# First norm of a hybrid layer: four selecting matmuls in a row, later strips recorded between the first products, twelve idle matmuls

## The chip, the cores and the metric

The kernel runs on one core of one Trainium2 chip. The metric is the device time of one execution in microseconds, the median of the runs shown. A profile of one further execution gives the rows used here.

## The reference

One layer of a bidirectional hybrid model works on 640 tokens of width 1024: 128 of a prompt and 512 of a sample. All matrices are float32. What matters for this change is the beginning:

```python
def layer(x, mod, p, lru_h0, gla_s0, rows):
    sh1, sc1, g1, sh2, sc2, g2 = jnp.split(mod, N_MOD, axis=-1)
    ng = p['norm_g']
    h = rmsnorm(x, ng[0]) * (1.0 + sc1) + sh1
    m, s_lru, s_gla = token_mix(h, p, lru_h0, gla_s0, rows)
    x = x + g1 * rmsnorm(m, ng[1])
    h = rmsnorm(x, ng[2]) * (1.0 + sc2) + sh2
    f = jnp.square(jax.nn.relu(h @ p['mlp_w1'])) @ p['mlp_w2']
    x = x + g2 * rmsnorm(f, ng[3])
```

Here `mod` is `silu(c) @ w_mod + b_mod`, once with the prompt's conditioning vector and once with the sample's; `w_mod` is 1024 by 6144. `token_mix` begins with `z = h @ p['w_in']` (1024 by 7200); its first 1024 columns feed a convolution and a recurrence.

## The kernel before, in words

**Layout.** The normed input h lies transposed, features on partitions, in eight column blocks k of 128 features by 640 tokens. Every product is made of three float32r matmuls, so h is kept as a high part (tile HH) and a remainder (tile HL), and every weight block as `whi` (a cast on ScalarE) and `wlo` (a subtraction on VectorE).

**The first norm.** Each of the five token tiles is loaded, squared and summed on ScalarE, scaled on VectorE, and transposed on TensorE into the tiles `xnT`. Then each column block k needs a scale column `a1` and a shift column `sh1` for both conditioning vectors. They come from two strips of 256 columns of `w_mod` for every two blocks, a "pair" n: `mod_load` loads a strip as four tiles `modw` of 256 KB, `mod_pair(n)` multiplies them with the conditioning vectors in sixteen matmuls (two rows of the profile each, as every float32 matmul), copies the sums to the tile `rw`, and gathers the columns with four selecting matmuls against `sel`, each followed by an add on VectorE into `a1` or `sh1`. `make_h(k)` scales block k (128 tokens on VectorE, 512 on ScalarE) and splits it into HH and HL.

**The first unit.** The input projection starts with three column blocks of `w_in` together (`N_FIRST`), with k as the outer loop: `first_part(k)` issues the products of block k for all three, 6 matmuls of 320 columns each. The three accumulate in two `dense` tiles and one `aux` tile of PSUM; there are two of each kind. `prep` loads weights (1 MB for two blocks, at most two such loads open) and splits them.

**The order.** Nothing is issued as it is written. A recorder keeps all operations with their dependencies; `order` is a list scheduler over all engines and the DMA queue, with a cost for each operation. An engine that comes free takes, among the instructions that are ready by the plan, the one of the lowest rank, which is the number of its recording less `rec.ahead`; it does not wait for one that will be ready soon. Weight splits are recorded with `rec.ahead = SPLIT_AHEAD` (50). A PSUM tile counts as one region, so that an engine's access waits for another engine's earlier accesses anywhere in the tile. The plan fixes the order on each engine; on the chip, each engine works through it and waits on semaphores. `startup` records the first norm after the letters of `MIX`: x a token tile's transposes, l the load of a strip, d and D weight loads, m a pair, p the first weight splits, h two blocks of h.

Of the kernel before, what the change touches and what calls it, by code (L numbers as in the profile page):

```python
# [39 lines left out]
POOL_OUT = (5,)  # L40
G2_FROM = 6
N_WARM = 24

EARLY = "xxxrxxmm"
MIX = "XdllxxxxxDllmphllmhmhmh"
N_FIRST = 3


# [6 lines left out]
def _dims(ap):  # L57
    n = 1
    for _, k in ap.ap[1:]:
        n *= k  # L60
    return n
# [48 lines left out]
class Recorder:  # L110
# [114 lines left out]
    def order(self):  # L225
# [20 lines left out]
        table, dma_free, seq, out, busy = None, 0.0, 0, [], {}  # L246
# [3 lines left out]
        while len(out) < len(ops):  # L250
            best = None
            for e in engs:
                if avail[e]:
                    t = free[e]
                elif future[e]:
                    t = max(free[e], future[e][0][0])
                else:
                    continue
                if best is None or t < best[0]:
                    best = (t, e)  # L260
            assert best, "no instruction can go on"
            t, e = best
            while future[e] and future[e][0][0] <= t:
                i = heapq.heappop(future[e])[1]
                heapq.heappush(avail[e], ops[i].rank)
            if e == "ACT" and table is not None:
                r = min(avail[e], key=lambda r: r[0] + (self.SWITCH_AGE if ops[r[1]].table not in (None, table) else 0))
                avail[e].remove(r)
                heapq.heapify(avail[e])
            else:  # L270
                r = heapq.heappop(avail[e])
            i = r[1]
            o = ops[i]
            wait, block = t, None
            fresh = [nm for nm in o.tiles if nm not in got]
            for tag in {self.tile_of[nm] for nm in fresh}:
                mine = [nm for nm in fresh if self.tile_of[nm] == tag]
                before = due[tag].index(max(mine, key=rank.get)) + 1
                if len(slots[tag]) < before:
                    block = tag  # L280
                else:
                    wait = max(wait, heapq.nsmallest(len(mine), slots[tag])[-1])
            if block:
                held[block].append(i)
                continue
            if wait > t:
                heapq.heappush(future[e], (wait, i))
                continue
            for nm in fresh:
                tag = self.tile_of[nm]  # L290
                got.add(nm)
                due[tag].remove(nm)
                heapq.heappop(slots[tag])
                for j in held[tag]:
                    heapq.heappush(future[ops[j].eng], (t, j))
                held[tag] = []
            us = o.us
            if o.table and o.table != table:
                us += self.SWITCH_US
                table = o.table  # L300
            if e == "PE":

                w = int(t / self.WINDOW_US)
                if busy.get(w - 1, 0.0) < 0.375 * self.WINDOW_US:
                    us *= 2
                if _dims(o.kw["out"] if "out" in o.kw else o.args[0]) >= 64:
                    busy[w] = busy.get(w, 0.0) + o.us
            o.at, o.seq = t, seq
            seq += 1
            free[e] = t + us  # L310
            o.done = t + us
            if o.name == "dma_start":
                dst = o.kw["out"]
                size = dst.ap[0][1] * _dims(dst) * 4
                onchip = o.kw["in_"].space == bass.MemoryType.SB
                dma_free = max(dma_free, t + us + 0.6) + size / 360e3
                o.done = dma_free + (1.25 if onchip else 0.9)
            out.append(o)
            for u in o.users:
                u.ready = max(u.ready, o.done + self.lag(e, u.eng))  # L320
                u.waits -= 1
                if not u.waits:
                    heapq.heappush(future[u.eng], (u.ready, u.idx))
            for nm in o.tiles:
                left[nm] -= 1
                if not left[nm]:
                    tag = self.tile_of[nm]
                    heapq.heappush(slots[tag], o.done + 0.1)
                    for j in held[tag]:
                        heapq.heappush(future[ops[j].eng], (t, j))  # L330
                    held[tag] = []
# [60 lines left out]
def tile_hybrid_layer(  # L392
# [7 lines left out]
    rec = Recorder(nc)  # L400
    V, A, PE, G, SP = (Port(rec, e) for e in ("DVE", "ACT", "PE", "POOL", "SP"))
# [13 lines left out]
    def t_(name, dt=F32):  # L415
        return rec.tile(tp, N_T, [128, TW], dt, name, "t")
# [4 lines left out]
    def dense():  # L421
        return rec.tile(psd, 2, [128, 2, 512], F32, "dense", "d")

    def aux():
        return rec.tile(psa, 2, [128, 2, 512], F32, "aux", "a")
# [14 lines left out]
    def copy(e, dst, src):  # L440
        A.copy(dst, src) if e == "A" else by[e].tensor_copy(dst, src)
# [15 lines left out]
    ident = consts.tile([128, 128], F32, name="ident")  # L457
# [19 lines left out]
    def load_rows(rows, q):  # L477
        for dst, r0, n, src in rows:
            q.dma_start(out=dst[r0:r0 + n, :], in_=src)
# [40 lines left out]
    ps = aux()  # L520
    for _ in range(N_WARM):
        PE.matmul(ps[:, 0, 0:128], ident, ident, start=True, stop=True)
# [19 lines left out]
    ps = aux()  # L542
# [6 lines left out]
    sel = consts.tile([128, 2], F32, name="sel")  # L549
# [82 lines left out]
    def mod_pair(n):  # L632


        ps = aux()

        for m in (1, 0):
            for r in (1, 0):
                for j in (3, 2, 1, 0):
                    k = 4 * r + j  # L640
                    PE.matmul(ps[32 * j:32 * (j + 1), m, 0:256], cst32[:, k, :], modw[2 * n + m][k // 2][:, k % 2, :],
                              start=r == 1, stop=r == 0)
        rw = t_("rw")
        A.copy(rw[:, 0:512].rearrange("p (m c) -> p m c", m=2), ps[:, :, 0:256])
        for m in range(2):
            for i in range(2):
                k = 2 * n + i
                pc = ps[:, m, 256 + 2 * i:258 + 2 * i]
                PE.matmul(pc, rw[:, 256 * m + 128 * i:256 * m + 128 * (i + 1)], sel, start=True, stop=True)
                if m:  # L650
                    V.tensor_scalar(cols["sh1"][:, :, k], pc, bm(0, k), None, op0=OP.add)
                else:
                    V.tensor_scalar(cols["a1"][:, :, k], pc, bm1[:, k:k + 1], ng(0, k), op0=OP.add, op1=OP.mult)

    xnT = []
    HH = rec.tile(big, 1, [128, 8, T], F32R, "HH", "hh")
# [8 lines left out]
    def make_h(k):  # L665
        x = xnT[k]
        for e, i, sl in zip(MH_ENG, range(2), (slice(0, 128), slice(128, T))):
            scaled(e, x[:, sl], x[:, sl], cols["a1"][:, i, k:k + 1], cols["sh1"][:, i, k:k + 1])
        copy(MH_ENG[2], HH[:, k, :], x[:, 0:T])
        by[MH_ENG[3]].tensor_tensor(HL[:, k, :], x[:, 0:T], f32(HH[:, k, :]), op=OP.subtract)  # L670
# [37 lines left out]
    def startup():  # L708
        ps = aux()
        PE.transpose(ps[:, 0, 0:80], v2[0:80, :], ident[0:80, 0:80])  # L710
        V.tensor_copy(C2, ps[:, 0, 0:80])
        V.tensor_scalar(bm1, bmv(1), 1.0, None, op0=OP.add)
        for t in range(NT):
            x_norm(t)
        load_rows(rows_etc, G)
        ps = aux()
        PE.transpose(ps[:, 0, 0:114], v1[0:114, :], ident[0:114, 0:114])
        V.tensor_copy(C1, ps[:, 0, 0:114])
        nm = nx = nh = 0
        for s_ in MIX:  # L720
            if s_ == "l":
                modw.append(mod_load(len(modw)))
            elif s_ == "m":
                mod_pair(nm)
                nm += 1
            elif s_ == "X":
                xnT.extend(t_(f"xnT{k}") for k in range(KT))
            elif s_ == "p":
                prep(0, 0, 0)
            elif s_ == "h":  # L730
                for k in (2 * nh, 2 * nh + 1):
                    make_h(k)
                nh += 1
            elif s_ in "dD":
                do_loads(1 if s_ == "d" else 2)
            else:
                x_T(nx, dense())
                nx += 1


    def fm_mm(ps, piece, xh, xl, c0, c1, ks, k_all=KT):
# [69 lines left out]
    def first_part(k):  # L811
        if k == 0:
            first_ps.extend([dense(), dense(), aux()])
        for u, p in enumerate(pzx[0:N_FIRST]):
            fm_mm(first_ps[u], p, hh, hl, 0, T, (k,))

# [1029 lines left out]
```

## Time and profile before

| | us |
|---|---|
| median of three runs | 1134.96 |
| lowest, highest run | 1134.83, 1137.45 |
| the profiled execution | 1134.4 |
| its span, first to last instruction | 1132.6 |

The profile is of one execution. Busy times count the instructions that the profiler saw on an engine; the end of a matmul is modelled, and matmuls overlap in the pipeline. All operations are issued by one helper line, L343, so that rows are told apart by their tiles.

### The profile page before, as it was taken

How to read it: one execution, taken by the hardware profiler on the slowest of the kernel's cores; microseconds unless marked ns; L12 is line 12 of the kernel's file. 1: busy time of each engine (PE TensorE's matmuls, PEld its weight loads, DVE VectorE, ACT ScalarE, POOL GpSimd, SP SyncE). 2: the span in 40 equal slices, each digit the busy share in tenths (PEclk: the TensorE clock that was granted, in tenths of full speed). 3: DMA queues.
4: the chain of work that ended last, by engine and by line, in shares of the span. 5: the costliest groups of instructions: out<-in, count | busy, mean ns of one | idle time of the engine just before them, and what ended most of it. 6: DMA issues, size and time to landing. Idle time of an engine off the chain costs nothing.

```text
span 1132.6 us, 17807 instructions
## 1 busy us (share of the span) xinstructions
PE 1106.1 (98%) x7020; PEld 1039.9 (92%) x7020; DVE 847.7 (75%) x1359; ACT 615.7 (54%) x998; POOL 78.7 (7%) x151
## 2 busy tenths in 40 slices
PE   6999999999999999999999999999999999999997
PEld 5799899999999999999999888888998988889896
DVE  4686885968474738628997569997779989987767
ACT  5377989895575758512443258754434433333452
POOL 3136103000000000000000021000000000000001
PEclk8999999999999999999999999999999999999999
DMA  9835436241321212226544456322233333222522
GB/s 293 269 73 152 123 83 176 69 132 38 95 75 57 75 57 75 90 76 235 176 158 168 143 196 207 124 76 75 75 129 128 101 124 134 94 75 75 154 88 93
DMA packets 104475, 136.94 MB, mean 121 GB/s; under 512 B 8178, under 2 KB 78020, under 8 KB 104392
## 3 DMA queue, kind: packets, MB, share of 16 engines
q1 hardware_dynamic: 102200, 133.65, 38.0%
q0 software_dynamic: 2048, 1.90, 0.7%
q8 instruction: 55, 0.90, 0.3%
q10 hardware_dynamic: 144, 0.26, 0.1%
q14 instruction: 28, 0.23, 0.1%
HBM read 121.61 MB, written 6.31 MB: 113 GB/s over the span
## 4 chain that ended last, share of the span: by engine, by line
PE 81%; DVE 6%; ACT 6%; DMA 4%; issue 2%; SPq 0%; POOL 0%; DVEq 0%; POOLq 0%; ACTq 0%
PE dense L343 55%; PE aux L343 26%; DVE i L343 2%; DMA modw<-in_w_mod_dram 1%; DVE th L343 1%; ACT L343 1%; DMA i<-r 1%; DVE wlo L343 1%; DMA raw<-in_w_in_dram 1%; ACT r L343 1%; ACT whi L343 1%; ACT th L343 1%; DMA xb<-in_x_sample_dram 0%; ACT L342 0%; DVE ab L343 0%
## 5 line engine op out<-in xcount | busy, mean ns | idle before, releaser
L343 ACT CAST whi<-raw 128x1024 fp32r<-128x1024 f32 (+2 forms) x173 | 167.0, 969 | 290.3 <-PE aux L343 140.3
L343 DVE TENSOR_TENSOR wlo<-raw,whi 128x1024 fp32r<-128x1024 f32 (+1 forms) x168 | 190.2, 1133 | 75.9 <-ACT whi L343 74.9
L343 PE MATMUL dense<-HH,whi 128*128 128x320 f32 x768 | 177.7, 311 | 0.2 <-ACT vc L343 0.2
L343 PE MATMUL dense<-HL,whi 128*128 128x320 f32 x768 | 175.9, 309 | 0.0
L343 PE MATMUL dense<-HH,wlo 128*128 128x320 f32 x752 | 172.4, 309 | 0.0
L343 PEld LDWEIGHTS dense<-HH,whi 128*128 128x128 f32 x768 | 128.2, 188 | 1.9 <-issue 0.6
L343 PEld LDWEIGHTS dense<-HL,whi 128*128 128x128 f32 x768 | 128.6, 188 | 0.0
L343 PEld LDWEIGHTS dense<-HH,wlo 128*128 128x128 f32 x752 | 125.9, 188 | 0.0
L343 PE MATMUL dense<-wlo,ah 128*128 128x512 f32 (+1 forms) x288 | 113.0, 392 | 0.0
L343 PE MATMUL dense<-whi,ah 128*128 128x512 f32 (+1 forms) x288 | 113.0, 392 | 0.0
L343 PE MATMUL dense<-whi,al 128*128 128x512 f32 (+1 forms) x288 | 112.9, 392 | 0.0
L343 DVE SCALAR_TENSOR_TENSOR mac<-mw,cst,mac 128x512 f32<-128x512 f32 x112 | 78.1, 746 | 0.0
L343 PE MATMUL aux<-H2H,whi 128*128 128x320 f32 (+1 forms) x240 | 74.8, 311 | 0.0
L343 PE MATMUL aux<-H2L,whi 128*128 128x320 f32 (+1 forms) x240 | 74.7, 311 | 0.0
L343 PE MATMUL aux<-H2H,wlo 128*128 128x320 f32 (+1 forms) x240 | 74.6, 311 | 0.0
L343 PEld LDWEIGHTS dense<-whi,al 128*128 128x128 f32 x288 | 54.1, 188 | 12.5
L343 PEld LDWEIGHTS dense<-whi,ah 128*128 128x128 f32 x288 | 54.1, 188 | 10.3
L343 PEld LDWEIGHTS dense<-wlo,ah 128*128 128x128 f32 x288 | 54.1, 188 | 10.2
L343 ACT CAST whi<-s 128x512 fp32r<-128x512 f32 x42 | 26.0, 620 | 67.2 <-PE aux L343 62.9
L343 PE MATMUL aux<-f,whi 128*128 128x320 f32 x224 | 59.4, 308 | 0.0
L343 DVE TENSOR_TENSOR fa<-fa,dense 128x512 f32<-128x512 f32 x66 | 45.3, 686 | 17.8 <-PE dense L343 17.6
L343 PE MATMUL aux<-f,wlo 128*128 128x320 f32 x168 | 51.9, 309 | 0.0
(334 smaller groups left out, 2496.3 us busy)
## 6 DMA issues: line engine op xcount, KB each, us to landing
raw<-in_mlp_w_dram SPq DMA_DIRECT2D x34, 1024.0 KB, 5.0
raw<-in_w_in_dram SPq DMA_DIRECT2D x24, 1024.0 KB, 5.4
mw<-in_w_mod_dram SPq DMA_DIRECT2D x64, 256.0 KB, 5.2
modw<-in_w_mod_dram SPq DMA_DIRECT2D x32, 256.0 KB, 6.3
raw<-in_w_out_dram SPq DMA_DIRECT2D x8, 1024.0 KB, 4.8
i<-r SPq DMA_DIRECT2D x32, 160.0 KB, 2.4
raw<-in_w_in_dram SPq DMA_DIRECT2D x8, 512.0 KB, 4.7
raw<-in_lru_up_dram SPq DMA_DIRECT2D x4, 1024.0 KB, 5.0
```

The source lines that it names most:

```text
L343: getattr(eng[o.eng], o.name)(*o.args, **o.kw)
```

## The change

`mod_pair` issues its four selecting matmuls in a row, and the four adds after them, ordered by block. From the strip copy to the last add its operations are recorded 150 ahead of their place. For pair 0, twelve matmuls of the copied strip with the identity follow the selecting ones; they write a PSUM tile that nobody reads. `make_h` is recorded 150 ahead as well. Pairs 1 to 3, with their two blocks of h each, are no longer recorded in `startup`, but in `first_part` before the products of k = 2, 4 and 6. The planner's rate for loads becomes 275 KB per us while its DMA clock is under 14 us and 350 after that, instead of 360.

```diff
+N_KEEP = 12
+MOD_AHEAD = 150
-MIX = "XdllxxxxxDllmphllmhmhmh"
+MIX = "XdllxxxxxDllmphll"
...
-                dma_free = max(dma_free, t + us + 0.6) + size / 360e3
+                dma_free = max(dma_free, t + us + 0.6) + size / (275e3 if dma_free < 14 else 350e3)
...
+        rec.ahead = MOD_AHEAD
         rw = t_("rw")
         A.copy(rw[:, 0:512].rearrange("p (m c) -> p m c", m=2), ps[:, :, 0:256])
-        for m in range(2):
-            for i in range(2):
-                k = 2 * n + i
-                pc = ps[:, m, 256 + 2 * i:258 + 2 * i]
-                PE.matmul(pc, rw[:, 256 * m + 128 * i:256 * m + 128 * (i + 1)], sel, start=True, stop=True)
+        pcs = [ps[:, m, 256 + 2 * i:258 + 2 * i] for m in range(2) for i in range(2)]
+        for n_, pc in enumerate(pcs):
+            PE.matmul(pc, rw[:, 128 * n_:128 * (n_ + 1)], sel, start=True, stop=True)
+        if n == 0:
+
+            keep = aux()
+            for _ in range(N_KEEP):
+                PE.matmul(keep[:, 0, 0:128], rw[:, 0:128], ident, start=True, stop=True)
+        for i in range(2):
+            for m in range(2):
+                k, pc = 2 * n + i, pcs[2 * m + i]
                 if m:
                     V.tensor_scalar(cols["sh1"][:, :, k], pc, bm(0, k), None, op0=OP.add)
                 else:
                     V.tensor_scalar(cols["a1"][:, :, k], pc, bm1[:, k:k + 1], ng(0, k), op0=OP.add, op1=OP.mult)
+        rec.ahead = 0
...
             elif s_ == "m":
-                mod_pair(nm)
-                nm += 1
+                mod_pair(0)
...
             elif s_ == "h":
-                for k in (2 * nh, 2 * nh + 1):
+                rec.ahead = MOD_AHEAD
+                for k in range(2):
                     make_h(k)
-                nh += 1
+                rec.ahead = 0
...
+    def next_pair(n):
+        mod_pair(n)
+        rec.ahead = MOD_AHEAD
+        for k in (2 * n, 2 * n + 1):
+            make_h(k)
+        rec.ahead = 0
...
     def first_part(k):
         if k == 0:
             first_ps.extend([dense(), dense(), aux()])
+        if k in (2, 4, 6):
+            next_pair(k // 2)
         for u, p in enumerate(pzx[0:N_FIRST]):
             fm_mm(first_ps[u], p, hh, hl, 0, T, (k,))
```

## Rows read from the trace of the kernel before

**Rows 1.** The page: busy time, share of the span, instructions.
```profile
PE 1106.1 (98%) x7020; PEld 1039.9 (92%) x7020; DVE 847.7 (75%) x1359; ACT 615.7 (54%) x998; POOL 78.7 (7%) x151
```

**Rows 2.** Windows: stretch, length, busy us by engine, granted clock, DMA share, GB/s.
```profile
0.00:33.00 33.00, 21.83 (x164) 17.37 (x164) 16.47 (x56) 18.32 (x53) 9.79 (x37) 0.84 0.97 301
33.00:62.40 29.40, 29.03 (x237) 26.01 (x234) 17.16 (x36) 11.11 (x17) 8.72 (x17) 1.00 0.67 209
80.00:200.00 120.00, 117.30 (x839) 116.68 (x838) 88.98 (x126) 107.05 (x134) 35.27 (x71) 1.00 0.50 134
```

**Rows 3.** Timeline, 20 to 33 us: start, duration, instruction, idle time before it.
```profile
20.32 1.93 PE L343 MATMUL aux<-modw,cst 128*32 128x256 f32 x32
...
22.63 1.99 ACT L343 CAST whi<-raw 128x1024 fp32r<-128x1024 f32 x2 [0.75 <-DMA raw<-in_w_in_dram]
...
24.52 0.58 ACT L343 COPY rw<-aux 128x512 f32<-128x512 f32 x1
...
25.15 0.38 PE L343 MATMUL aux<-sel,rw 128*128 128x2 f32 x2 [2.90 <-ACT rw L343]
25.98 0.28 DVE L343 TENSOR_SCALAR a<-aux,bm,C 128x2 f32<-128x2 f32 x1
...
28.16 0.35 DVE L343 TENSOR_SCALAR xnT<-xnT,a,sh 128x128 f32<-128x128 f32 x1
...
28.18 0.59 PE L343 MATMUL aux<-sel,rw 128*128 128x2 f32 x2 [0.32 <-DVE sh L343]
28.22 1.71 ACT L343 ACTIVATE xnT<-xnT,sh,a 128x512 f32<-128x512 f32 x2 [3.12 <-DVE sh L343]
...
29.07 0.49 DVE L343 CAST HH<-xnT 128x640 fp32r<-128x640 f32 x1
...
29.55 3.47 PE L343 MATMUL aux<-modw,cst 128*32 128x256 f32 x32 [0.78 <-DMA modw<-in_w_mod_dram]
...
32.95 0.56 PE L343 MATMUL dense<-HH,whi 128*128 128x320 f32 x2
```

**Rows 4.** Windows around two changes of the clock; the third number from the end.
```profile
25.75:26.00 0.25, 0.00 (x0) 0.00 (x0) 0.25 (x2) 0.00 (x0) 0.00 (x0) 0.79 1.10 356
32.50:32.75 0.25, 0.25 (x8) 0.00 (x0) 0.00 (x0) 0.21 (x1) 0.00 (x0) 0.56 1.10 344
```

**Rows 5.** Timeline, 32 to 41 us: weight block three, pair 2, products of k=2.
```profile
32.54 1.05 ACT L343 CAST whi<-raw 128x1024 fp32r<-128x1024 f32 x1 [2.60 <-DMA raw<-in_w_in_dram]
...
33.62 1.23 DVE L343 TENSOR_TENSOR wlo<-raw,whi 128x1024 fp32r<-128x1024 f32 x1 [1.80 <-ACT whi L343]
...
38.56 1.93 PE L343 MATMUL aux<-modw,cst 128*32 128x256 f32 x32
40.43 0.56 PE L343 MATMUL dense<-HH,whi 128*128 128x320 f32 x2
```

**Rows 6.** The chain that ended last: start, length, what.
```profile
23.36 9.15 DMA raw<-in_w_in_dram
...
59.88 1.76 PE dense L343 x12
...
62.51 10.56 PE dense L343 x72
...
92.31 6.12 DMA i<-r
```

**Rows 7.** Tile rw, 20 to 60 us: duration min/median/max in ns.
```profile
L343 PE MATMUL aux<-sel,rw x32: 165/251/374, 25.2 to 51.3; 128*128 128x2 f32 x32
```

**Rows 8.** Windows of the identity matmuls at the start, TensorE alone.
```profile
2.05:5.47 3.42, 3.42 (x16) 1.00 0.74 243
5.47:8.87 3.40, 3.40 (x32) 1.00 0.94 294
```

**Rows 9.** The page: DMA issues, count, size, median us to landing.
```profile
i<-r SPq DMA_DIRECT2D x32, 160.0 KB, 2.4
```

More of the change, by code (lines that the diff above doesn't have):

```diff
@@ L718, in startup @@
         V.tensor_copy(C1, ps[:, 0, 0:114])
-        nm = nx = nh = 0
+        nx = 0
         for s_ in MIX:
```

## Prediction, written before the change was run

> **What bounds the kernel now.** I read the page first: TensorE is busy for 98% of the span [rows 1], so a change at the front can only be worth time that TensorE loses there. The table of windows says where: 11 us are lost before 33 us, and 0.4 us between 33 and 62.4 us, in which the first three blocks of the input projection are made; the later stretch with the long recurrence loses 2.7 us of 120 [rows 2]. The most that anything in the first norm can give back is therefore a handful of microseconds out of 1134.
>
> The timeline shows how the 33 us end [rows 3]. The sixteen matmuls of strip pair 0 (two rows each) start at 20.32 and end at 22.25. ScalarE then casts two weight blocks, and only at 24.52 copies the strips to SBUF. From 25.15 to 28.18 the four selecting matmuls alternate with the adds on VectorE, 1.01 us a round. The column blocks HH 0 and 1 of the normed input are made from 29.07. TensorE does pair 1 in 3.47 us, and the first product starts at 32.95. The clock explains the 3.47: the granted clock changes inside the slices at 25.75 and 32.50 [rows 4] and was half in between, after TensorE had stood from 22.25 to 25.15; pair 2, at full clock, takes 1.93 us [rows 5]. The chain of waits shows the second weight load landing 9.15 us after 23.36, at 32.51, and the first unit of three blocks ending where the 72 dense matmuls begin, at 62.5 [rows 6].
>
> **The change, part by part.**
>
> *The strip copy.* It gets precedence over the casts. By the planner's constants the last strip load of pair 0 is due 3.0 us before the first weight block (1 MB at 350 KB per us), and sixteen matmuls fit in between, so I expect the copy before the casts: 22.3 instead of 24.52, ending 22.9 (0.58). The casts then run from 22.85 to 24.85 (1.99 for two, [rows 3]). If it stays behind them, this 2.2 us is lost again.
>
> *Selecting in one go.* A selecting matmul costs two rows of 0.25 us median, overlapping [rows 7]; I take 0.25 each, between 0.19 and 0.38. Four end at 23.95. The adds (0.28, then closely behind one another, so 0.25 each) end at 25.0, where the alternation would have taken four rounds of 1.01. The added wait: the first add stands behind all four selections, 0.75 us later than before relative to the first of them. What is queued behind it on VectorE are the two scalings and the casts, all of which need it anyway.
> The Trainium skill (PSUM — Partial Sum Buffer, "PSUM bank collisions raise a hardware error") has TensorE's writes and another engine's reads of one bank kept apart by semaphores. The alternation in rows 3 agrees with it; by that rule the 0.75 us cannot be avoided, and without it each pair would come 0.75 us sooner.
>
> *The twelve idle matmuls.* The trace has their like at the start: 16 rows in 3.42 us, then 32 rows in 3.40 [rows 8]. At two rows each that is 0.43 us at half and 0.21 us at full clock. Twelve fill 2.6 us (23.95 to 26.5) or 5.1 us. They depend on the copied strips alone and stand ahead of every product. Their cover is the time until HH 0 exists. With the second cast in front, ScalarE scales block 0 from 24.85 to 25.7 (1.71 us for two). VectorE is free after adds and scalings (0.35 each) at 25.75; one weight remainder, 1.22 us, is ready by then, and the planner fills an engine with whatever is ready, so I put it first. HH 0 ends at 27.5 (cast 0.49). At full clock the idle matmuls cost nothing; at half clock throughout they would end at 29.1 and cost 1.6 us. Best start of products 26.5, mine 27.5.
> Rows 4 show the clock falling after TensorE stood still and rising after pair 1 had kept it at work; the new order leaves it standing 0.7 us before the selections and 1.0 us before the products, where it stood 2.9 at a stretch. The Trainium skill (TensorE: Matmul & The Clock Gate, "What's actually happening") says that the default state is throttled and activity releases it. By that rule the idle matmuls hold full clock, and the sum is as below; without it, the first products at half clock until 29.2 would make it 0.9 us worse.
>
> *Pairs 1 to 3 moved between the products.* Their 16 matmuls each have no precedence; they now queue behind blocks k=0,1, then k=2,3, then k=4,5. No DMA is moved: all strip loads and the weight loads are issued in the same order as before, so SP and POOL carry what they carried. The work of TensorE up to the end of the first unit: 144 products (12 in 1.76 us, [rows 6]) are 21.1 us, three pairs 5.8, twelve selections 3.0: 29.9. By the other way, the 29.03 busy us of 33 to 62.4 plus pair 1's 1.93, it is 31.0. I take 30.4. Starting at 27.5 without a wait, the unit would end at 57.9 instead of 62.5. The waits eat most of that:
> - Block three's weights land at 32.51 and the cast takes 1.05 [rows 5]. Until then TensorE has 24 products (3.5) and pair 1 (1.9): it runs dry at 33.0.
> - Pair 1's chain starts at 33.0 as well: copy 0.6, selections 1.0, two adds 0.5, ScalarE scaling 0.86, HH cast 0.49, and links: HH 2 at 36.5 to 37. On VectorE two weight remainders of 1.22 us (block three's and four's) become ready just when the adds and the cast do; each that is taken first delays HH 2 by as much. None gives 36.6, both 39.3; I take one, 38.2. TensorE's cover is block three's k=0,1 (1.76) and the selections (0.9), so it waits 38.2 − 33.0 − 2.7 = 2.5 us (1.3 at best, 3.6 at worst).
> - Pair 2 starts only after k=2,3; its chain of 3.5 us is covered by the selections (0.9) and pair 3's matmuls (1.9): 0.7 us of waiting. Pair 3's chain is under k=4,5 (5.3 us): nothing.
>
> Sum: 27.5 + 30.4 + 2.5 + 0.7 = 61.1 against 62.5: 1.4 us gained. Best ends together: 26.5 + 29.9 + 1.35 + 0.7 = 58.5, 4.0 gained. With the copy still behind the casts, products start at 31, pair 1's chain meets no remainders (0.8 us of waiting) and it is 31 + 30.4 + 0.8 + 0.7 = 62.9: 0.4 lost; with half clock on top, 1.3 lost.
>
> *The planner's DMA rate* (275 KB per us early, 350 instead of 360 later) costs no instruction. It moves every load's due time in the plan, a 1 MB load by 0.08 us, and can reorder any later stage; see the fourth rival.
>
> What is gained at 62.5 should reach the end: the chain of waits runs on from there through products and the recurrence, and nothing in it is tied to a fixed time.
>
> **The rivals.** The profiled execution took 1134.4 us, 0.6 below the median of the three timed (1134.96). About 0.3%, 3.4 us, is what a measurement of this kernel can tell from no change.
> 1. *Everything lines up*: adds and HH casts ahead of the remainders, full clock throughout. For it: the precedence of 150 against 50 for the splits. Against it: precedence only decides between instructions that are ready together. 1134.4 − 4.0 = 1130.4.
> 2. *It does not do what it says*: the copy still follows the casts, and TensorE's wait moves from before the products to between them. 1134.4 + 0.4 = 1134.8.
> 3. *The clock falls all the same at about 26 us*, as in rows 4, and the idle matmuls take 5.1 us instead of 2.6: with the copy late, 1134.4 + 1.3 = 1135.7. It decides if a stop from 22.25 to 24.5, with the copy late, has the effect that the stop to 25.15 had.
> 4. *A later stage is replanned* (the one that ends slower). In the recurrence the chain hangs on gate transfers from SBUF to SBUF: one in the chain takes 6.12 us [rows 6], while the median of the 32 is 2.4 [rows 9]; the difference of 3.7 us is about what a 1 MB weight load ahead of it takes. One more of them behind a load: 1134.4 − 1.4 + 3.7 = 1136.7, and 1138.5 if the front gives nothing. One fewer: 1129.3. It decides where SP's order puts a weight load before such a transfer. For it: all due times move. Against it: the shift is 0.08 us per load.
>
> **How the numbers follow.** Forecast (1.4 gained, 1133.0): 0.45. Rival 1: 0.20; rival 2: 0.13; rival 3: 0.07; rival 4: 0.15, of which 0.06 is the good side and 0.09 the bad. Faster by over 0.3% means under 1131.6: rival 1 and the good side of rival 4, 0.26. Slower by over 0.3% means above 1138.4: the bad side of rival 4 with some gain lost, 0.09. The rest, 0.65, is within. The range of 1130.3 to 1136.7 runs from rival 1 to the bad side of rival 4; the forecast's own range, with none or both of the remainders in front, is 1131.5 to 1134.2.
>
> **What would show it.** Right: the strip copy before the first weight cast, at 22.3 to 22.5; four selecting matmuls with no VectorE instruction between them; 12 idle matmuls in about 2.6 us; granted clock full across 25.8; the first product at 26.5 to 27.5; a hole of 1 to 3 us on TensorE between 33 and 39, ended by HH; the unit's end 1 to 2 us before 62.5. Wrong: idle matmuls at 0.43 us each, the copy after the casts, HH 2 before 36.5 (then it is rival 1), or a first unit that ends early while the end of the run does not follow.

## The result and the profile after

The changed kernel took 1145.62 us in the median (1143.19 to 1147.83, four runs); the kernel before, run beside it, took 1134.89 (1133.98 to 1137.45). The ratio is 1.0084, 95% interval 1.0064 to 1.0103: it is slower by some 10 us, where 1.4 us of gain was forecast and slower by over 0.3% had 0.09 of the chance. In the last group of runs below it was 1.0059 (1.0038 to 1.0080). The profiled execution shown here took 1147.83 us, the slowest of its four.

The page of the kernel after has the line that answers to [rows 1]: TensorE's share falls by one point although it is busy 10 us longer.

```profile
PE 1116.3 (97%) x7044; PEld 1048.7 (91%) x7044; DVE 846.2 (74%) x1359; ACT 615.1 (54%) x998; POOL 78.2 (7%) x151
```

The table of windows of the kernel after, with the columns of [rows 2], first over the same stretches and then cut at the events of the first unit:

```profile
0.00:33.00 33.00, 26.41 (x185) 23.47 (x185) 16.05 (x56) 18.28 (x53) 9.52 (x35) 0.90 0.97 302
33.00:62.40 29.40, 23.52 (x201) 18.49 (x201) 12.61 (x31) 8.11 (x13) 5.01 (x12) 1.00 0.65 202
80.00:200.00 120.00, 114.00 (x772) 112.59 (x771) 90.44 (x127) 100.70 (x132) 31.06 (x64) 0.97 0.49 130
...
28.20:69.32 41.12, 34.96 (x266) 29.07 (x267) 19.12 (x40) 11.31 (x17) 9.88 (x23) 0.96 0.61 191
...
39.77:51.97 12.20, 10.63 (x98) 8.11 (x99) 4.74 (x12) 2.75 (x5) 1.86 (x3) 1.00 0.80 244
51.97:62.24 10.27, 7.59 (x58) 6.63 (x55) 3.60 (x11) 1.98 (x3) 3.15 (x10) 1.00 0.19 58
62.24:69.32 7.08, 7.08 (x38) 7.08 (x39) 3.72 (x6) 2.60 (x6) 4.87 (x11) 0.76 0.12 32
```

The head is fuller: TensorE is busy for 26.41 us of the first 33, where it was 21.83 [rows 2]; 2.92 us of that are the idle matmuls. What was won there, and more, is lost in the next stretch: 5.9 us of 29.4 are empty, where 0.4 were. The timeline of the kernel after shows how, with the columns of [rows 3]:

```profile
21.57 1.93 PE L345 MATMUL aux<-modw,cst 128*32 128x256 f32 x32
23.57 0.58 ACT L345 COPY rw<-aux 128x512 f32<-128x512 f32 x1 [0.44 <-PE aux L345]
24.06 1.99 ACT L345 CAST whi<-raw 128x1024 fp32r<-128x1024 f32 x2
24.21 1.05 PE L345 MATMUL aux<-sel,rw 128*128 128x2 f32 x8 [0.70 <-ACT rw L345]
25.13 2.92 PE L345 MATMUL aux<-ident,rw 128*128 128x128 f32 x24
25.38 0.28 DVE L345 TENSOR_SCALAR a<-aux,bm,C 128x2 f32<-128x2 f32 x1 [3.65 <-PE aux L345]
28.20 0.86 PE L345 MATMUL dense<-HH,whi 128*128 128x320 f32 x4
...
31.29 0.63 PE L345 MATMUL aux<-modw,cst 128*32 128x256 f32 x6
33.22 1.91 PE L345 MATMUL aux<-modw,cst 128*32 128x256 f32 x26
35.17 0.59 ACT L345 COPY rw<-aux 128x512 f32<-128x512 f32 x1 [1.88 <-PE aux L345]
36.74 1.22 DVE L345 TENSOR_TENSOR wlo<-raw,whi 128x1024 fp32r<-128x1024 f32 x1 [2.19 <-ACT whi L345]
39.22 0.49 DVE L345 CAST HH<-xnT 128x640 fp32r<-128x640 f32 x1
39.77 0.85 PE L345 MATMUL dense<-HH,whi 128*128 128x320 f32 x4 [1.62 <-DVE HH L345]
40.85 0.62 PE L345 MATMUL aux<-modw,cst 128*32 128x256 f32 x2
46.00 1.93 PE L345 MATMUL aux<-modw,cst 128*32 128x256 f32 x30
48.62 1.05 PE L345 MATMUL aux<-sel,rw 128*128 128x2 f32 x8 [0.69 <-ACT rw L345]
50.55 1.50 PE L345 MATMUL aux<-modw,cst 128*32 128x256 f32 x22 [0.87 <-PE aux L345]
57.45 1.05 PE L345 MATMUL aux<-modw,cst 128*32 128x256 f32 x10
58.54 0.58 ACT L345 COPY rw<-aux 128x512 f32<-128x512 f32 x1 [6.79 <-PE aux L345]
61.69 0.49 DVE L345 CAST HH<-xnT 128x640 fp32r<-128x640 f32 x1
62.24 1.32 PE L345 MATMUL dense<-HH,whi 128*128 128x320 f32 x4 [2.01 <-DVE HH L345]
```

The reader is to see three pairs of strips that are each torn in two. Pair 1 has 6 rows at 31.29 and 26 after more products, at 33.22. Pair 2 has 2 rows at 40.85, and 30 at 46.00, behind the products of k=2 and 3. Pair 3 has 22 rows at 50.55, and the last 10 at 57.45, behind the products of k=4 and 5. Only behind a pair's last row can its strip be copied, and from there to the next HH it takes 3.7 to 4.6 us (57.45 + 1.05 = 58.50 to 62.18 for pair 3). TensorE soon has nothing else to do. In the kernel before, no pair is torn: pairs 1 and 2 stand whole in [rows 3] and [rows 5], and so does pair 3:

```profile
45.18 1.93 PE L343 MATMUL aux<-modw,cst 128*32 128x256 f32 x32
```

The chain of waits shows the end of the first unit, where the 72 dense matmuls of [rows 6] begin, at 69.3 instead of 62.5:

```profile
69.32 10.56 PE dense L345 x72
```

### The profile page after: what moved, and what is told of

The parts are those of the page before. It is cut to its first block, busy times and chain, and to the rows that moved or that the text cites. A ratio compares the mean times of both kernels' runs of the same rounds, so it can differ in the third digit from the quotient of the medians.

```text
span 1146.1 us, 17866 instructions
## 1 busy us (share of the span) xinstructions
PE 1116.3 (97%) x7044; PEld 1048.7 (91%) x7044; DVE 846.2 (74%) x1359; ACT 615.1 (54%) x998; POOL 78.2 (7%) x151
## 4 chain that ended last, share of the span: by engine, by line
PE 80%; ACT 8%; DVE 6%; issue 3%; DMA 2%; POOL 0%; DVEq 0%; SPq 0%; POOLq 0%; ACTq 0%
PE dense L345 53%; PE aux L345 27%; DVE i L345 2%; ACT L345 1%; ACT th L345 1%; DVE th L345 1%; ACT r L345 1%; ACT whi L345 1%; DVE wlo L345 1%; DMA i<-r 1%; DMA r<-r 1%; DMA w2raw<-in_gla_w_dram 1%; ACT L344 1%; ACT junk L345 0%; DVE ab L345 0%
```

## The experiments

In the table below the end of the first unit is read from the copy of its last PSUM tile to the tile `zp` (some 0.4 us behind the start of the 72 matmuls), and the recurrence from there to the last copy into the tile `nst`, both of one profiled execution. Behind that copy, every kernel takes 866.5 to 868.0 us more. The last column is the ratio to the kernel before, run beside it. The times in the expectations are counted from the 1134.9 us of the first comparison; beside the experiments the kernel before took 1137.1 to 1138.2, so the ratios decide.

| kernel | unit's end | recurrence | ratio, 95% interval |
|---|---|---|---|
| before, first profile | 62.9 | 202.3 | |
| before again (e13) | 63.4 | 207.0 | 1.0001, 0.9986 to 1.0016 |
| after, first profile | 69.8 | 208.3 | 1.0084, 1.0064 to 1.0103 |
| after again (e14) | 69.6 | 206.0 | 1.0059, 1.0038 to 1.0080 |
| e1 pairs ahead | 61.2 | 200.8 | 0.9929, 0.9914 to 0.9943 |
| e2 place back | 63.6 | 205.6 | 1.0005, 0.9990 to 1.0019 |
| e3 no idle matmuls | 73.0 | 205.8 | 1.0089, 1.0074 to 1.0104 |
| e4 rates alone | 66.2 | 205.5 | 1.0030, 1.0020 to 1.0041 |
| e5 rate back | 72.5 | 205.9 | 1.0079, 1.0064 to 1.0094 |
| e6 one go alone | 62.6 | 205.4 | 1.0003, 0.9993 to 1.0014 |
| e7 recorded one block earlier | 63.0 | 200.2 | 0.9961, 0.9948 to 0.9975 |
| e8 e1 with the old rate | 60.0 | 204.1 | 0.9961, 0.9948 to 0.9974 |
| e9 355 as the rate | 64.2 | 205.5 | 1.0007, 0.9994 to 1.0021 |
| e10 e1 without idle matmuls | 61.1 | 199.8 | 0.9933, 0.9913 to 0.9953 |
| e11 pair 3 ahead | 65.4 | 205.2 | 1.0013, 1.0000 to 1.0027 |
| e12 unit held up | 68.6 | 208.1 | 1.0092, 1.0067 to 1.0117 |
| e15 held up a third | 66.5 | 207.8 | 1.0027, 1.0010 to 1.0043 |
| e16 e1 held up | 66.4 | 201.2 | 0.9998, 0.9982 to 1.0014 |

**e1, the pairs' matmuls ahead as well.** The one line that gives precedence stands above the matmuls of the pair instead of below them.

```diff
+        rec.ahead = MOD_AHEAD
         for m in (1, 0):
             ...
                               start=r == 1, stop=r == 0)
-        rec.ahead = MOD_AHEAD
         rw = t_("rw")
```

> The changed kernel, with the sixteen matmuls of each pair recorded 150 ahead as well. Order theory (the loss is the pairs' matmuls queueing behind the products of the blocks before, so that TensorE stands empty while copy, adds and cast follow): the first unit ends at 59 to 62 us instead of 69.3, and the total falls by at least 7 us, to 1133 to 1139. Rate theory (the loss comes from the planner's new DMA rates, which reorder the recurrence): the first unit gains, the later 4 to 6 us stay, 1139 to 1141. Idle-matmul theory (the loss is the twelve extra matmuls and what they push back): no change, 1143 to 1147.

Measured: 1129.84 us (1129.30 to 1130.36) beside 1138.22 of before, ratio 0.9929. The loss turns into a gain, and this kernel beats both others. Its timeline, TensorE alone:

```profile
26.77 0.85 PE L345 MATMUL dense<-HH,whi 128*128 128x320 f32 x4
...
29.57 1.93 PE L345 MATMUL aux<-modw,cst 128*32 128x256 f32 x32
...
36.04 0.57 PE L345 MATMUL aux<-HH,wlo 128*128 128x320 f32 x2 [1.39 <-DVE wlo L345]
...
40.70 1.93 PE L345 MATMUL aux<-modw,cst 128*32 128x256 f32 x32
...
47.33 1.93 PE L345 MATMUL aux<-modw,cst 128*32 128x256 f32 x32
```

All three pairs run whole, and no wait for HH is left; the longest wait is for the weight remainder of block three. The first product also comes earlier than in the changed kernel (26.77 instead of 28.20); from there to the unit's end it is 34.4 us instead of 41.6. So the torn pairs were the cause of the lost unit: their new place without precedence explains it. The gain over the kernel before is mostly another matter, the shorter recurrence (see rival 4 below).

**e2, pairs 1 to 3 recorded in `startup` again**, the rest of the change kept.

```diff
-MIX = "XdllxxxxxDllmphll"
+MIX = "XdllxxxxxDllmphllmhmhmh"
...
-        if k in (2, 4, 6):
-            next_pair(k // 2)
```

> The changed kernel with pairs 1 to 3 recorded in startup again; selections in one go, idle matmuls, precedence 150 and the new DMA rates stay. Order theory: 1131 to 1136, first unit ending at 60 to 62.5. Rate theory: 1138 to 1141, with the first unit as early but the recurrence as slow as in the changed kernel. Idle-matmul theory: over 1142.

Measured: 1138.64 us, ratio 1.0005. The unit ends at 63.6, some 1 us later than the order theory had it. The loss goes away with the place; the change's other parts together bring nothing that can be measured.

**e3, without the twelve idle matmuls** (`N_KEEP = 0`; only work that nobody reads is left out).

> The changed kernel without the twelve idle matmuls. Order theory: same time within 2 us, 1143 to 1148, since HH 0 ends at 28.15 us and the idle matmuls at 28.05; if the clock then falls near 26 us, up to 1 us worse. Idle-matmul theory: 3 us or more faster, under 1142.5. Rate theory: no change.

Measured: 1148.04 us, ratio 1.0089. The unit ends 3.3 us later in its profile than in the two of after (69.7). Its ratio lies inside the interval of the first comparison and above that of the second. The idle matmuls did not cause the loss; whether they save something in this order (without them the granted clock is 0.68 from 28.5 to 33.8 us, and pair 1 is torn in three) these times do not tell.

**e4, the planner's rates alone**, on the kernel before; **e5, the changed kernel with the old rate**.

```diff
-                dma_free = max(dma_free, t + us + 0.6) + size / 360e3
+                dma_free = max(dma_free, t + us + 0.6) + size / (275e3 if dma_free < 14 else 350e3)
```

> The kernel before with nothing but the planner's new DMA rates. Rate theory: 4 to 6 us slower, 1139 to 1141. Order theory: within 2 us of before, 1133 to 1137, with only some reordering.

> The changed kernel with the old DMA rate of 360. Order theory: the first unit still ends at 67 to 70 us, because the pairs' matmuls still queue behind the products; the total stays at least 5 us over before. Rate theory: most of the loss is gone, within 3 us of before. If the recurrence (from the first unit's end to the last state column, 203 us before, 209 in the changed kernel) comes back to 203 with the unit still late, the loss is the sum of both.

Measured: e4 1141.56 us, 1.0030; e5 1146.48, 1.0079. Alone, the rates cost 3.4 us, which lies between the two theories of e4: the first product comes at 29.5, yet pair 1 still runs at half clock (3.64 us from 30.85, the granted clock being 0.52 in 28 to 33 us) and the unit ends at 66.2. Taken out of the changed kernel, they give nothing back; in e5 the unit even ends at 72.5. So they are not the cause of the loss, and their price depends on the plan that they meet (e8 below has the other sign).

**e6, the four selecting matmuls in one go alone**, on the kernel before.

> The kernel before with the four selecting matmuls in one go and nothing else. Each pair's chain loses three round trips of about 1 us less what the first add waits longer. Theory that the selections were on the path of the start: HH 0 about 2 us earlier, first unit ending 1 to 2.5 us before 62.5, total 1 to 3 us under before. Rival, that they were covered by the products and by the wait for data: within 1 us of before.

Measured: 1137.28 us, 1.0003. The first product comes at 27.99 instead of 32.95, and the unit still ends at 62.6. Two products run, and then pair 1, which stood ahead of the products before; it takes 3.64 us at half clock (3.47 before; granted clock 0.50 from 27.99 to 33.28):

```profile
27.99 0.90 PE L343 MATMUL dense<-HH,whi 128*128 128x320 f32 x2 [2.01 <-DVE HH L343]
29.64 3.64 PE L343 MATMUL aux<-modw,cst 128*32 128x256 f32 x32 [0.74 <-DMA modw<-in_w_mod_dram]
```

TensorE is busy for 21.83 us of the first 33, exactly as before [rows 2]: it waits elsewhere for what it no longer waits for in the selections. The copy follows the casts here, as the forecast's second rival had it, and the outcome is that rival's, in a part of the change by itself.

**e7, pairs recorded one block earlier** in the changed kernel, before the products of k = 1, 3 and 5.

```diff
-        if k in (2, 4, 6):
-            next_pair(k // 2)
+        if k in (1, 3, 5):
+            next_pair((k + 1) // 2)
```

> The changed kernel with each pair recorded one block of k earlier (before the products of k = 1, 3, 5 instead of 2, 4, 6), its matmuls still without precedence. Order theory as a dose: each chain then has 2.65 us more of products behind its matmuls to cover it, so that the holes in front of HH 2, 4 and 6 (1.6, 1.6 and 2.7 us and the half clock that follows) all but go; first unit ending at 61 to 64, total 4 to 11 us under the changed kernel. If precedence itself matters and not the place in the queue: no better than 1142.

Measured: 1132.57 us, 0.9961. The pairs are still torn (10 and 22 rows, 4 and 28, 12 and 20), but each is whole one block before it is needed, and the waits for HH come to 1.5 us. What counts is that a block of products is left to cover the chain.

**e8, e1 with the old rate**, and **e10, e1 without the idle matmuls**.

> The changed kernel with the pairs' matmuls ahead, and the old DMA rate of 360. Theory that the better order of the first unit alone makes the gain of 8 us over before: within 2 us of the run with the new rates. Theory that the recurrence is dealt a good or a bad order by every new plan: first unit as early (59 to 62), but the recurrence 202 to 209 us, and the total 0 to 8 us worse than with the new rates.

> The changed kernel with the pairs' matmuls ahead and without the twelve idle matmuls: what these are worth in the good order. If they only hold the clock: products from about 26.8 us at half clock until about 30 to 33 us, first unit 1 to 2 us later than the 61.2 with them. If they are worth nothing: first unit within 0.5 us. The recurrence may move by some us either way with the new plan.

Measured: e8 1132.57 us, 0.9961; e10 1130.06, 0.9933. With the old rate the unit ends as early as in no other kernel (60.0), but the recurrence is 3.3 us longer. In this order the idle matmuls are worth nothing that can be measured, although they do what they are put there for. The table of windows of e1, then of e10 (the third number from the end is the granted clock):

```profile
26.00:32.60 6.60, 6.17 (x61) 4.60 (x59) 3.73 (x6) 1.30 (x3) 0.00 (x0) 1.00 1.09 358
32.60:36.00 3.40, 2.05 (x16) 1.78 (x15) 2.37 (x8) 3.16 (x4) 0.00 (x0) 1.00 1.11 351
36.00:40.00 4.00, 3.96 (x16) 3.96 (x17) 3.40 (x5) 0.00 (x0) 0.00 (x0) 0.57 1.08 346
```

```profile
26.00:32.60 6.60, 5.31 (x33) 3.50 (x37) 3.96 (x6) 0.68 (x1) 0.00 (x0) 0.50 1.09 358
32.60:36.00 3.40, 3.40 (x33) 2.90 (x25) 1.60 (x2) 2.48 (x3) 0.00 (x0) 0.98 1.10 348
36.00:40.00 4.00, 3.73 (x33) 3.10 (x36) 3.81 (x11) 1.52 (x2) 0.00 (x0) 1.00 1.10 349
```

With them TensorE runs at full clock from 26 us, has used up its ready products by 34.6, stands, and then pays with half clock from 36 to 40 us. Without them it is slow first, and just in time for block three's weights.

**e9, 355 KB per us as the only rate**, on the kernel before.

> The kernel before with 355 instead of 360 for the planner's DMA rate, a change without any purpose. Theory that each new plan deals the recurrence another order: the recurrence (first unit's end to last state column) leaves its 202.3 us, for 204 to 208 as in the other replanned kernels, and the total moves by 1 to 4 us. Rival, that the early rate of 275 or the order of the first unit does it: recurrence and total stay within 1 us of before.

Measured: 1138.86 us, 1.0007: a shift of the due times by itself costs nothing that can be measured. The recurrence of 205.5 us is what the theory asked for, but the kernel before itself has 207.0 in a second profile (e13 below), so this tells nothing.

**e11, precedence for pair 3's matmuls alone**, in the changed kernel.

```diff
+        rec.ahead = MOD_AHEAD if n == 3 else 0
         for m in (1, 0):
```

> The changed kernel with only pair 3's matmuls ahead. Order theory: the hole in front of HH 6 (2.7 us of standing, then 3.3 us at half clock, worth 1.7) goes, the holes in front of HH 2 and 4 stay; first unit ending 4 to 5 us before the changed kernel's 69.8, so at 65 to 66. If the three chains are one and the same bottleneck, the hole only moves: within 1.5 us of 69.8.

Measured: 1138.27 us, 1.0013. The unit ends at 65.4, that is 4.3 us before that of the changed kernel; e1 brings the other 4.2 (to 61.2). Of the 4.3, 1.1 are an earlier first product (27.14 instead of 28.20). Counted from the first product, pair 3's precedence takes 3.3 us off the unit and all of e1 7.2, so that about half of the lost unit was pair 3, for which the prediction had nothing. It could have been more: pair 3 now runs whole, but in 3.62 us, with a granted clock of 0.53 from 49.70 to 53.30.

**e12, the kernel before with its first unit held up.** Pair 3's sixteen matmuls are issued three times more (the result is the same, the planner does not know of it), so that plan and order are those of before.

```diff
             getattr(eng[o.eng], o.name)(*o.args, **o.kw)
+            if o.idx in self.again:
+                for _ in range(3):
+                    for q in self.again[o.idx]:
+                        nc.tensor.matmul(*q.args, **q.kw)
```

> The kernel before, same plan and same order, with pair 3's sixteen matmuls issued four times in a row (same result; 5.8 us more on TensorE that the plan does not know of). Theory that the recurrence's length belongs to the plan: first unit ends at 68 to 69, recurrence still 202 to 203 us, total 5 to 6.5 us slower. Rival, that a late first unit itself lengthens the recurrence (by running into transfers at fixed times): recurrence 205 to 209, total 9 us or more slower.

Measured: 1147.63 us, 1.0092, with a unit that ends 5.7 us later than in the first profile of before. The recurrence of 208.1 looked longer than the 202.3 of before, as that of the changed kernel had. That would have meant that lateness feeds on itself in a fixed order. Whether it does is what the last four kernels ask.

**e13 and e14, both kernels once more, e15, a third of the delay, and e16, the delay of e12 in e1.**

> The kernel before once more, profiled beside the other three. Theory (a late first unit lengthens the recurrence): as in the first profile, the unit's end at 62 to 64 us and the recurrence from there to its last normalised state 201 to 203.5 us. Rival (the first profile of before was a short one): 204 to 206.5 us.

> The changed kernel once more. Theory: the unit's end at 69 to 72 us, the recurrence 205.5 to 209 us, at least 2.5 us longer than that of before in this group. Rival: the recurrence within 1.5 us of that of before in this group, so that the whole loss lies ahead of the unit's end.

> Before with pair 3's sixteen matmuls issued twice (once more instead of three times more; the result is the same), about 1.9 us of delay in the first unit. If a delay is only passed on: 1.5 to 2.3 us slower than before. If it grows in proportion, as 5.7 grew to 10.4: 3 to 4 us slower.

> The changed kernel with the pairs' matmuls recorded ahead too, and pair 3's sixteen issued four times (the result is the same), about 5.7 us of delay. If a late first unit lengthens the recurrence whatever the plan: the recurrence 204 to 207 us instead of 200.8, the total 9 to 12 us over that kernel's without delay, 0 to 4 us slower than before. If this plan has slack: 5 to 6.5 us over it, 1.5 to 3 us faster than before.

Measured: e13 1138.15 us, e14 1144.52, e15 1140.93, e16 1136.62, beside 1137.11 of before. The two ends of the stage, read from the tiles `zp` and `nst` (times from and to at the end of the line), for e13, e14 and e16 in turn:

```profile
L343 DVE COPY zp<-aux x1: 283/283/283, 63.4 to 63.4; 128x128 f32<-128x128 f32 x1
L343 DVE COPY nst<-i x16: 126/129/148, 124.5 to 270.4; 128x1 f32<-128x1 f32 x16
```

```profile
L345 DVE COPY zp<-aux x1: 282/282/282, 69.6 to 69.6; 128x128 f32<-128x128 f32 x1
L345 DVE COPY nst<-i x16: 122/128/148, 131.3 to 275.6; 128x1 f32<-128x1 f32 x16
```

```profile
L346 DVE COPY zp<-aux x1: 282/282/282, 66.4 to 66.4; 128x128 f32<-128x128 f32 x1
L346 DVE COPY nst<-i x16: 126/128/135, 129.8 to 267.6; 128x1 f32<-128x1 f32 x16
```

My theory that a late unit lengthens the recurrence fell, and its rival stands: in this second profile the kernel before has a recurrence of 207.0 us (0.5 beyond even the rival's range), the changed one 206.0. The same program differs by 4.7 us between two profiled executions, and the first of before was a short one. e16 agrees: 5.2 us of delay in the unit leave e1's recurrence at 201.2 (it was 200.8), against the theory's 204 to 207. Its time is 1136.62 us, 0.9998 of before. This lies between its two cases: against e1's 0.9929 it is 0.0069, or 7.8 us with an uncertainty of some 2.4 (both intervals' half widths, 1.6 and 1.8 us, added in squares). e15's unit ends 3.1 us after that of e13 and its ratio gives 3.1 us (1.1 to 4.9), which does not tell its two cases apart. A delay of the first unit reaches the end in full, then. The kernels with the latest units agree: e3's and e5's end 9.1 to 10.1 us after those of before, their times are 10.1 and 9.0 us longer, and their recurrences are 205.8 and 205.9. Whether a little more is added in some orders, as e12's 10.5 us (7.6 to 13.3) for a unit later by 5.2 to 5.7 suggests, stays open.

## Why the prediction was wrong

**What was right.** The copy of pair 0's strip came ahead of the casts. The four selections took 1.05 us where four rounds of 1.01 us had been, with no VectorE instruction between them. The idle matmuls took 2.92 us (2.6 forecast) at full clock, so rivals 2 and 3 did not occur at this place. The first weight remainder ran before HH 0 (26.52), as assumed. The first product came at 28.20, 0.7 us after the forecast's, as pair 0's own matmuls began at 21.57 instead of 20.32. The first add stands at 25.38, behind the fourth selection (25.26), the 0.75 us that the prediction left in. That the Trainium skill (PSUM — Partial Sum Buffer, "PSUM bank collisions raise a hardware error") has TensorE's writes and another engine's reads of one bank kept apart agrees with this. The prediction's "cannot be avoided" went further than that: the recorder takes a whole PSUM tile as one region, so the 0.75 us show its rule, and no run tried a finer one.

**The step that failed** is the one on the moved pairs, and in it above all "Pair 3's chain is under k=4,5 (5.3 us): nothing". The prediction had said itself that the pairs' matmuls "have no precedence" and "queue behind blocks", and then took each pair as one piece, with pair 3 running whole ahead of k=4,5, to cover pair 2's chain, though it is recorded behind them. The planner's rule, by which an engine takes the ready instruction of the lowest rank, gives another picture: as soon as HH of the next block is ready, the 36 products of its two k go before what is left of the pair, and the remainder of the pair waits behind all of them. Then the cover that the sum counted on, k=4,5 for pair 3's chain, is spent before the chain begins. From 28.20 to 69.32 us the terms were, against the forecast's:

| term | forecast | measured |
|---|---|---|
| wait for HH 2 (pair 1) | 2.5 | 1.62 |
| pair 2 | 0.7 | 1.57 (12.20 − 10.63) |
| pair 3 | 0 | 2.68 (10.27 − 7.59) |
| other waits | 0 | 0.29 (6.16 empty in all) |
| half clock, 62.24 to 69.32 | 0 | 1.80 (7.08 − 36 products at 1.76 for 12) |
| three pairs' matmuls | 5.8 | 7.64 (each torn: 0.63 + 1.91, 0.62 + 1.93, 1.50 + 1.05) |
| the rest of the work | 24.6 | 25.5 (34.96 − 1.80 − 7.64) |

With the start 0.7 us later, that is 8.2 us: 69.3 instead of 61.1. Pair 1's chain was about as long as estimated (35.13 to 39.71, 4.6 us against 5.2); it only began at 35.1 instead of 33.0. Pair 3 costs 4.5 us of waiting and half clock; e11, which gives precedence to pair 3 alone, brings back 3.3 of them behind the first product, while its own pair 3 runs at half clock.

**The clock** was looked for at the wrong place. TensorE worked for 1.55 us of the 4.2 between 58.0 and 62.2 us, and behind that the granted clock was 0.53, near the lower of its two levels, from 62.2 to 65.5:

```profile
58.00:62.20 4.20, 1.55 (x14) 0.98 (x9) 1.73 (x7) 1.94 (x3) 0.00 (x0) 1.00 0.00 0
62.20:65.50 3.30, 3.26 (x13) 3.27 (x14) 2.56 (x4) 0.67 (x2) 1.16 (x2) 0.53 0.00 0
```

The Trainium skill (TensorE: Matmul & The Clock Gate, "What's actually happening") has activity as what releases a throttle that is there by default; these rows agree, and so do the windows of e1 and e10. But a held clock brings time only if the products are not short of weights or HH anyway, as e1 and e10 show (1129.84 us with it, 1130.06 without).

**From the unit to the end** the prediction was right: what happens at 62.5 reaches the end (e12, e15, e16). The unit, later by 6.9 us in the first pair of profiles and 6.2 in the second, stands beside 9.5 us (7.3 to 11.7) of time in the first comparison and 6.7 (4.3 to 9.1) in the second. The first is some 3 us more than the unit accounts for; in the first pair of profiles the recurrence is longer by 6.0 us as well, in the second it is shorter by 1.0.

**Rival 4**, a later stage that is replanned, is not needed for the loss: the two kernels' recurrences overlap (202.3 and 207.0 against 208.3 and 206.0). That it added to the first comparison is neither shown nor ruled out. Its price of 3.7 us set a step of the chain (6.12) against a median from issue to landing (2.4); by the second measure none of the 32 transfers took more than 4.1 us in that trace. Its good side came true in another kernel. e1, e7, e10 and e16 have recurrences of 200 to 201 us, and e1's gain of 8.1 us is more than its unit's 1.7 to 2.2. The waits in the recurrence show where, here from 62 to 280 us, first in e13, then in e1, which has no row for the second of them:

```profile
DVE i L343 <- DMA i<-r: 12.4, 7, 3.9
PE aux L343 <- ACT r L343: 4.8, 3, 3.2
```

```profile
DVE i L345 <- DMA i<-r: 3.3, 3, 1.8
```

The transfers of the gates from SBUF to SBUF are waited for 9 us less than in e13, and 5.5 less than in the first profile of before (8.8). e16, with 3.9 us of this wait in spite of its late unit, shows that this belongs to the order that was planned and not to the early start. Which instruction's place does it was not tried by itself; e8, whose 204.1 us come with 11.4 us of the first wait, differs from e1 only in the planner's rate.

**Slips in the working** that did not decide. With no remainder in front, HH 2 at 36.6 makes the wait 0.9 us and not 1.3. Rival 4 with no gain at the front is 1138.1; 1138.5 needs rival 2's loss as well. Its bad side has 0.09 of the chance as slower by over 0.3%, though its own 1136.7 lies within. In [rows 8] the granted clock is 1.00 in both windows, so that "half" was read there from the times of the rows alone. The 29.2 us until which the first products were to run at half clock stands in no row; in e10, without the idle matmuls, they did so until 32.5.

## What to carry to other kernels

Where a list scheduler orders an engine, work that is moved between other work must be given its rank as well as its place: a chain of one copy, four small matmuls, some adds and a cast (3.7 to 4.6 us here) has to begin one block of products before its result is needed, and without precedence the last of its matmuls begins when that block is over. When such a chain is costed, ask of each of its instructions what the planner may take first, not only of the first one. In this kernel, whose TensorE is busy for 98% of the time, a first unit that came later by 6 us made it slower by at least about that much, while a first product that came 5 us earlier (e6) was worth nothing, since other work only changed places with it.

## What was not expected of the hardware

One program's recurrence took 202.3 us in one profiled execution and 207.0 in another, with 8.8 and 12.4 us of waits for the same transfers; this is as large as the effect that was looked for, so one profile of each kernel could not tell where the loss arose. 6.6 us of half clock at the head (e10, granted clock 0.50 from 26 to 32.6 us) cost no time that could be measured: with the clock held there (e1), TensorE waited 1.39 us for block three's weights and then ran at a granted clock of 0.57 from 36 to 40 us.
